# A fifth token tile's normalised rows turned by VectorE and DRAM scratch instead of TensorE, with the turned rows of both halves in blocks of 32 tokens

## The chip, the cores and the metric

The kernel runs on one core of a Trainium2 chip (trn2). The time is device microseconds of one execution of the whole program; the time before is the median of three runs. A profiled execution, taken separately, gives the trace from which all rows below come.

## What is computed

One decoder layer on 1024 tokens (plus 16 meta tokens in front) of width 1024, float32. Cut to what matters here:

```
u = rmsnorm(h, g_pre_mix);  q, k, v, xr, yr = split(u @ w_in)
attn = sliding_window_attention(q, k, v);  rec = gelu(yr) * rg_lru(conv(xr))
h = h + rmsnorm(concat(attn, rec) @ w_out, g_post_mix)       # "output projection"
u = rmsnorm(h, g_pre_ffn)                                    # "second norm"
f = square(relu(u @ w_ff1)) @ w_ff2                          # d_ff = 4096
return h + rmsnorm(f, g_post_ffn)
```

The change concerns the second norm's result `u`, on its way from rows (a token per partition) to columns (a feature per partition), as the product with `w_ff1` needs it.

## The kernel before

**Products.** Each float32 product is made of three TensorE products of rounded parts (`mm3`, lines 123-133): high by high (line 125), high by low (line 130), low by high (line 131). The high part is a ScalarE cast and the low part a VectorE subtraction (`split`, lines 94-101: casts at line 96, subtractions at line 99). Both feed-forward products are done with a seven-product scheme on 2x2 blocks, so sums and differences of blocks of `u` and of the weights have to be formed first (`combine`, line 1029).

**The output projection and the second norm, lines 1136-1188.** The tokens go in eight tiles of 128 rows, t = 0 to 7. For each t, `out_mm` makes two TensorE banks; `out_norm` squares them on ScalarE (line 972), takes a root on GpSimd (`rstd_of`, lines 167-179), scales them on VectorE (line 978), adds x (line 981), writes h to the output (line 982, SyncE's DMA queue), and gets the second norm's factor (lines 984-985). `out_scale` then follows one or two tiles later (`scale_at`, line 1142).

- For t = 0 to 3, `u2_store` scales by the norm's factor and by `g_pre_ffn` in one VectorE instruction that also deals the columns out (line 930), turns the 32x32 blocks by a VectorE transpose (line 937), and stores 512 KB to a DRAM scratch `u2_dram` (line 938, SyncE's queue). `u2_read` (lines 940-945), one step of the loop later, reads it back in four loads of 128 KB into the four tiles `u2f[0]`, of shape [128, 16, 2, 32]: 16 blocks of 32 tokens, each with 2 feature chunks.
- For t = 4 to 7, `out_scale` scales the rows alone (line 991), and `u2_tiles` (lines 994-1017) turns them by eight TensorE transposes against an identity (line 1003). They go from PSUM to the four tiles `u2f[1]`, of shape [128, 2, 512], by four ScalarE instructions (line 1014) and two VectorE instructions (line 1008), which multiply by `g_pre_ffn`; for t = 6 ScalarE does all eight.

**After the turn.** `b11` and `b21` are the split parts of `u2f[0]` (lines 1183, 1186). `t_sums` (lines 1156-1161) forms `t3 = u2f[1][2+i] - u2f[1][i]` and `t2 = t3 + u2f[0][i]` and splits `t2` into `ot2`. It is called for tiles 4 and 5 (line 1178), 6 (line 1195) and 7 (line 1198). The function `rows` (lines 1031-1034) views a plain [128, 2, 512] tile by blocks of 32 tokens where the other operand is in blocks.

**The first feed-forward product.** `p1` and `p2` (lines 1146-1154) do the products that need only `u2f[0]`, for four blocks of weights. Then a loop over 16 blocks p of `w_ff1` begins (line 1224): `prep_a` (lines 1060-1083) loads two tiles of 512 KB by SyncE's queue (lines 1062 and 1064; `raw` and `a` or `d` tiles), forms sums (line 1029), and splits a part into `ws` and a part into `e` tiles; `product(ya[p], wa[p][1], ot2, ...)` (line 1229) uses `ot2`, and a store to DRAM scratch leaves by GpSimd's queue (line 1082).

**The order of the work.** A scheduler puts the instructions of each engine, and the DMA issues of SyncE, into one fixed order when the kernel is built; every engine then runs its own list in that order, waiting on semaphores. `behind` adds order constraints by hand. A wait therefore holds up all that stands behind it on that engine or queue. One tile pool has two `e` buffers (one holds `gmix_b` through this stage) and two `raw` buffers.

Of the kernel before, what the change touches and what calls it, by code (L numbers as in the profile page):

```python
# [9 lines left out]
F32 = mybir.dt.float32  # L10
F32R = mybir.dt.float32r
AF = mybir.ActivationFunctionType
ALU = mybir.AluOpType
# [3 lines left out]
P = 128  # L17
# [20 lines left out]
def hybrid_layer(  # L38
# [14 lines left out]
    dpool = ctx.enter_context(tc.tile_pool(name="dpool", bufs=1, space=DRAM))  # L53
# [4 lines left out]
    def slot(tag, shape, dt=F32):  # L58
        uid[0] += 1
        return slab.tile(shape, dt, tag=tag, name=f"{tag}{uid[0]}", bufs=bufs[tag])  # L60

    def pair(tag, shape):
        return slot(tag, shape, F32R), slot(tag, shape, F32R)

    def bank(tag, shape=(P, 512)):
        uid[0] += 1
        return ps.tile(list(shape), F32, tag=tag, name=f"ps_{tag}{uid[0]}")

    def f32(ap):
        return ap.bitcast(F32)  # L70
# [23 lines left out]
    def split(hi, lo, src, eng=None):  # L94
        if eng is None:
            nc.scalar.copy(hi, src)  # L96
        else:
            eng.tensor_copy(hi, src)
        low = nc.vector.tensor_tensor(lo, src, f32(hi), op=ALU.subtract).ins  # L99
        mark[0] = low.name  # L100
        return low


    mark = [None]

    def behind(name, *inss):
        for ins in inss:
            tc.add_manual_dep(
                ins, name,
                mybir.DependencyInfo(  # L110
                    mybir.DependencyClass.NoSync, mybir.DependencyReason.DATA
                ),
                reason="order",
            )
# [47 lines left out]
    g_mix_col, g_ffn_col = gcol[:, 0:8], gcol[:, 8:16]  # L162
# [368 lines left out]
    for h in range(2):  # L531
        r, o, m = HALF[h], HALF[1 - h], slice(P - NMETA, 2 * P)
# [62 lines left out]
    for b in range(2):  # L595
        pv = bank("pt", (P, 4, P))
        for i in range(4):
            o = NMETA + (4 * b + i) * P
# [319 lines left out]
    nc.scalar.dma_start(gmix_b, g_post_mix[0].partition_broadcast(P))  # L918
    t4_dram = dpool.tile([P, 2, 4, 512], F32, name="t4_dram")

    u2f = [[slot("c", [P, 16, 2, 32]) for _ in range(4)], [None] * 4]
    u2_dram = dpool.tile([4, 4, P, 2 * P], F32, name="u2_dram")
    gpre_b = slot("ws", [P, D])
    nc.scalar.dma_start(gpre_b, g_pre_ffn[0].partition_broadcast(P))

# [3 lines left out]
    def u2_store(t, h, rs, tmp):  # L929
        ins = nc.vector.scalar_tensor_tensor(  # L930
            tmp.rearrange("p (b k d) -> p k d b", b=4, k=KC), dealt(h), rs,
            dealt(gpre_b), op0=ALU.mult, op1=ALU.mult,
        ).ins
        if t < 3:
            behind(summed[t + 1], ins)
        y = slot("e", [P, D])
        nc.vector.transpose(y, tmp)
        nc.sync.dma_start(u2_dram[t].rearrange("a (d b) r -> (a d) (b r)", b=4), y)

    def u2_read(t):  # L940
        for q in range(4):
            nc.sync.dma_start(
                u2f[0][q][:, 4 * t : 4 * t + 4].rearrange("p a k t -> p a (k t)"),
                u2_dram[t, :, :, 64 * q : 64 * q + 64].rearrange("a p r -> p a r"),
            )

    def out_mm(t, po, kcs):
        half, o = t // 4, (t % 4) * P
        s = slice(o, o + P)
        for n in range(2):  # L950
            c = slice(512 * n, 512 * n + 512)
            for kc in kcs:
                ah, al = at[half][kc // 2]
                mm3(
                    po[n], (ah[:, kc % 2, s], al[:, kc % 2, s]),
                    (wo[kc][0][:, c], wo[kc][1][:, c]), kc == 0, kc == KC - 1,
                )

    def out_banks(t):
        tag = ("pt", "o", "acc", "s", "pt", "acc", "s", "pt")[t]  # L960
        return [bank(tag), bank(tag)]
# [23 lines left out]
        return h, xr, rstd_of([ssq2])  # L985

    def out_scale(t, h, xr, rs2):
        if t < 4:
            u2_store(t, h, rs2, xr)
            return None  # L990
        nc.vector.tensor_scalar(xr, h, rs2, None, op0=ALU.mult)
        return xr

    def u2_tiles(t, xn):
        half = t // 4
        if u2f[half][0] is None:
            u2f[half] = [slot("c", [P, 2, 512]) for _ in range(4)]
        o = (t % 4) * P
        for k4 in range(0, KC, 4):
            pt = bank("o", (P, 4, P))  # L1000
            for i in range(4):
                kc = k4 + i
                nc.tensor.transpose(pt[:, i, :], xn[:, kc * P : (kc + 1) * P], ident)
            for i in range(0, 4, 2):
                kc = k4 + i
                dst = u2f[half][kc // 2]
                if k4 and t != 6:
                    nc.vector.tensor_tensor(
                        dst[:, :, o : o + P], pt[:, i : i + 2, :],
                        g_ffn_col[:, kc : kc + 2].to_broadcast([P, 2, P]), op=ALU.mult,  # L1010
                    )
                    continue
                for n in range(2):
                    nc.scalar.activation(
                        dst[:, n, o : o + P], pt[:, i + n, :], AF.Copy,
                        scale=g_ffn_col[:, kc + n : kc + n + 1],
                    )

    w1v = w_ff1.rearrange("(b k p) c -> b p k c", b=2, p=P)

# [4 lines left out]
    def combine(dst, x0, x1, op):  # L1028
        return nc.vector.tensor_tensor(dst, x0, x1, op=op).ins  # L1029

    def rows(t_, c=slice(0, 512)):
        if len(t_.shape) == 4:
            return t_[:, c.start // 32 : c.stop // 32]
        return t_[:, :, c].rearrange("p k (g t) -> p g k t", t=32)

    def operand(tiles):
        pairs = []
        for t_ in tiles:
            hi, lo = pair("b", [P, 2, 512])
            if len(t_.shape) == 4:  # L1040
                split(rows(hi), rows(lo), t_)
            else:
                split(hi, lo, t_)
            pairs.append((hi, lo))
        return pairs

# [39 lines left out]
    def early(b, p0, hl, tag="raw"):  # L1086
        raw = slot(tag, [P, 2, 4, P])
        for k in range(2):
            w1_load(raw[:, k], b, p0 + k, 0, 1)
        split(*hl, raw)  # L1090
        return {p0 + k: (hl[0][:, k], hl[1][:, k]) for k in range(2)}
# [63 lines left out]

    def t_sums(c):
        for i in range(2):
            combine(t3[i][:, :, c], u2f[1][2 + i][:, :, c], u2f[1][i][:, :, c], ALU.subtract)
            combine(rows(t2[i], c), rows(t3[i], c), rows(u2f[0][i], c), ALU.add)
            hi, lo = ot2[i]  # L1160
            split(hi[:, :, c], lo[:, :, c], t2[i][:, :, c])

    for t in range(8):
        po = pos[t] if t < 4 else out_banks(t)
        out_mm(t, po, range(6 if t < 4 else 0, KC))
        if t > 5:
            u2_tiles(t - 2, xns[t - 2])
        if t == 7:
            t3 = [slot("a", [P, 2, 512]) for _ in range(2)]
            t2 = [slot("a", [P, 2, 512]) for _ in range(2)]  # L1170
            ot2 = [pair("b", [P, 2, 512]) for _ in range(2)]
        halfway[t] = out_norm(t, po)
        for k in scale_at[t]:
            xns[k] = out_scale(k, *halfway.pop(k))
        if 1 <= t <= 4:
            u2_read(t - 1)
        if t == 7:
            t_sums(slice(0, 2 * P))
            u2_tiles(6, xns[6])
        if t == 4:  # L1180
            a11_early.update(early(0, 0, pair("a", ESH)))
        if t == 5:
            b11 = operand(u2f[0][0:2])
            a12_early.update(early(1, 0, pair("ws", ESH)))
        if t == 6:
            b21 = operand(u2f[0][2:4])
            hl = slot("b", ESH, F32R), slot("e", ESH, F32R)
            a11_early.update(early(0, 2, hl))
# [3 lines left out]
        p1(p, a11_early[p])  # L1192
    for p in range(2):
        p2(p, a12_early[p])
    t_sums(slice(2 * P, 3 * P))
    wa[0] = prep_a(0)
    u2_tiles(7, xns[7])
    t_sums(slice(3 * P, 4 * P))
    urgent = mark[0]
    for p in range(2, 4):  # L1200
        p1(p, a11_early[p])
    p2(2, a12_early[2])
    ot3 = [pair("b", [P, 2, 512]) for _ in range(2)]
    for i in range(2):
        behind(urgent, split(*ot3[i], t3[i]))
    token_low = mark[0]
    wa[1] = prep_a(1, urgent)

# [1 line left out]
    def t_rest(k):  # L1210
        i = k % 2
        if k < 2:
            behind(mark[0], combine(rows(u2f[1][i]), rows(u2f[1][i]), u2f[0][i], ALU.subtract))
        elif k < 4:
            behind(mark[0], combine(rows(t2[i]), u2f[0][2 + i], rows(t2[i]), ALU.subtract))
        else:
            hl = pair("a", [P, 2, 512])
            late = mark[0]
            behind(late, split(*hl, t2[i]))
            for n in range(2):  # L1220
                nc.gpsimd.dma_start(t4_dram[:, n, 2 * i : 2 * i + 2, :], f32(hl[n]))

# [277 lines left out]
    for n, (i, q) in enumerate(steps):  # L1500
# [3 lines left out]
        if n + 1 < len(steps):  # L1504
            late = w_low[0]
# [55 lines left out]
```

## Time and profile before

| | us |
|---|---|
| median of 3 runs (949.52 to 950.42) | 950.23 |
| the profiled execution's own time | 949.03 |
| its span, first to last instruction | 947.3 |
| granted TensorE clock, share of full | 0.998 |

The page of the profile gives busy time by engine, the chain of work that ended last, and the costliest groups. The timeline gives instructions in order of time: start, duration, engine, line, operation, what is written and read (buffer numbers left out), and in square brackets how long the engine sat idle before and what released it. PE is TensorE, DVE VectorE, ACT ScalarE, POOL GpSimd, SPq SyncE's queue of DMA issues. A matmul's duration includes its pipeline: the distance from one start to the next is what it costs. Line numbers are those of the kernel before.

### The profile page before, as it was taken

The numbers are of one execution on the slowest core, as the hardware profiler recorded it, in microseconds if no ns is written. First come the engines' busy times: TensorE is split into PE (matmuls) and PEld (weight loads), VectorE is DVE, ScalarE is ACT, GpSimd is POOL, SyncE is SP. The second block draws the span as 40 slices with busy tenths as digits, with TensorE's granted clock in tenths as the row PEclk, the third lists the DMA queues.
The fourth block names the chain that finished last, engine by engine and source line by source line (L and its number), as shares of the span: only waits on it lengthen the run. The fifth ranks groups of instructions, "written<-read, shape, count | busy, mean of one in ns | idle before, by whom it ended". The sixth has DMA issues, their size and how long they took to land.

```text
span 947.3 us, 12174 instructions
## 1 busy us (share of the span) xinstructions
PE 937.9 (99%) x4584; PEld 784.8 (83%) x4584; DVE 664.4 (70%) x849; ACT 505.0 (53%) x844; POOL 135.9 (14%) x205
## 2 busy tenths in 40 slices
PE   9999999999999999999999999999999999999996
PEld 8999999878888878888888888888888888888885
DVE  6667788779977987665544465476667676779783
ACT  8546765569634664443655575654533443445441
POOL 4104437431021100010000000001111000001201
PEclk9999999999999999999999999999999999999999
DMA  8220011104259658574422363334777655537934
GB/s 273 57 68 23 24 45 45 45 23 141 82 194 273 200 180 283 188 258 134 156 89 89 111 215 120 109 111 114 198 170 178 206 179 192 194 126 209 238 64 89
DMA packets 97366, 134.91 MB, mean 142 GB/s; under 512 B 22230, under 2 KB 61158, under 8 KB 97308
## 3 DMA queue, kind: packets, MB, share of 16 engines
q1 hardware_dynamic: 87996, 108.64, 35.3%
q0 software_dynamic: 8880, 24.19, 11.9%
q10 hardware_dynamic: 432, 1.31, 0.4%
q8 instruction: 36, 0.59, 0.3%
q14 instruction: 22, 0.18, 0.1%
HBM read 112.55 MB, written 20.97 MB: 141 GB/s over the span
## 4 chain that ended last, share of the span: by engine, by line
PE 97%; DVE 1%; DMA 0%; ACT 0%; issue 0%; SPq 0%; DVEq 0%
PE ps_acc L125 12%; PE ps_acc L131 12%; PE ps_acc L130 12%; PE ps_pt L131 6%; PE ps_s L131 6%; PE ps_pt L125 6%; PE ps_pt L130 6%; PE ps_s L125 6%; PE ps_s L130 6%; PE ps_o L125 5%; PE ps_o L131 5%; PE ps_o L130 5%; PE ps_o L697 2%; PE ps_acc L282 1%; PE ps_s L629 1%; PE ps_s L633 1%
## 5 line engine op out<-in xcount | busy, mean ns | idle before, releaser
L99 DVE TENSOR_TENSOR ws<-raw,ws 128x1024 fp32r<-128x1024 f32 (+1 forms) x69 | 82.3, 1193 | 72.4 <-PE ps_o L130 23.1
L96 ACT CAST ws<-raw 128x1024 fp32r<-128x1024 f32 (+1 forms) x68 | 69.8, 1027 | 82.0 <-PE ps_o L130 33.6
L96 ACT CAST ws<-e 128x1024 fp32r<-128x1024 f32 x41 | 43.0, 1050 | 85.8 <-PE ps_o L130 38.2
L130 PE MATMUL ps_acc<-a,ws 128*128 128x512 f32 (+3 forms) x240 | 82.9, 346 | 0.0
L125 PE MATMUL ps_acc<-a,ws 128*128 128x512 f32 (+3 forms) x240 | 82.8, 346 | 0.0
L131 PE MATMUL ps_acc<-a,ws 128*128 128x512 f32 (+3 forms) x240 | 82.2, 343 | 0.0
L99 DVE TENSOR_TENSOR b<-b,b 128x1024 fp32r<-128x1024 f32 (+2 forms) x50 | 59.0, 1179 | 27.9 <-PE ps_o L130 22.6
L99 DVE TENSOR_TENSOR ws<-e,ws 128x1024 fp32r<-128x1024 f32 x41 | 50.2, 1223 | 31.7 <-ACT ws L96 18.4
L96 ACT CAST b<-b 128x1024 fp32r<-128x1024 f32 (+2 forms) x49 | 50.0, 1020 | 41.8 <-DVE b L1029 35.5
L684 POOL TENSOR_SCALAR_AFFINE_SELECT c<-c 128x512 fp32r<-128x512 f32 x64 | 55.0, 873 | 73.7 <-ACT c L96 64.2
L125 PEld LDWEIGHTS ps_acc<-a,ws 128*128 128x128 f32 x240 | 45.2, 189 | 4.3 <-issue 0.7
L131 PEld LDWEIGHTS ps_acc<-a,ws 128*128 128x128 f32 x240 | 45.2, 188 | 3.7 <-issue 0.2
L130 PEld LDWEIGHTS ps_acc<-a,ws 128*128 128x128 f32 x240 | 45.2, 188 | 3.6 <-issue 0.4
L131 PE MATMUL ps_acc<-ws,b 128*128 128x512 f32 (+1 forms) x120 | 46.3, 386 | 0.0
L130 PE MATMUL ps_acc<-ws,b 128*128 128x512 f32 (+1 forms) x120 | 46.2, 385 | 0.0
L125 PE MATMUL ps_acc<-ws,b 128*128 128x512 f32 (+1 forms) x120 | 46.0, 385 | 0.0
L125 PE MATMUL ps_pt<-ws,b 128*128 128x512 f32 x112 | 44.3, 395 | 0.0
L131 PE MATMUL ps_pt<-ws,b 128*128 128x512 f32 x112 | 44.2, 395 | 0.0
L130 PE MATMUL ps_pt<-ws,b 128*128 128x512 f32 x112 | 44.1, 394 | 0.0
L131 PE MATMUL ps_s<-ws,b 128*128 128x512 f32 x110 | 43.4, 394 | 0.0
L130 PE MATMUL ps_s<-ws,b 128*128 128x512 f32 x110 | 43.4, 394 | 0.0
L125 PE MATMUL ps_s<-ws,b 128*128 128x512 f32 x110 | 43.3, 394 | 0.0
(417 smaller groups left out, 2660.0 us busy)
## 6 DMA issues: line engine op xcount, KB each, us to landing
raw<-in_w_ff_dram SPq DMA_DIRECT2D x59, 512.0 KB, 3.9
e<-in_w_ff_dram SPq DMA_DIRECT2D x43, 512.0 KB, 3.5
a<-in_w_ff_dram SPq DMA_DIRECT2D x12, 512.0 KB, 6.0
s_dram<-a POOLq DMA_DIRECT2D x12, 512.0 KB, 4.1
raw<-in_w_in_dram SPq DMA_DIRECT2D x9, 512.0 KB, 3.6
c<-in_x_dram SPq DMA_DIRECT2D x8, 512.0 KB, 4.5
d<-in_x_dram SPq DMA_DIRECT2D x8, 512.0 KB, 3.4
out_dram<-raw SPq DMA_DIRECT2D x8, 512.0 KB
```

The source lines that it names most:

```text
L96: nc.scalar.copy(hi, src)
L99: low = nc.vector.tensor_tensor(lo, src, f32(hi), op=ALU.subtract).ins
L125: ins = nc.tensor.matmul(dst, lh, rh, start=start, stop=False, skip_group_check=True).ins
L130: nc.tensor.matmul(dst, lh, rl, start=False, stop=False, skip_group_check=True)
L131: last_mm[0] = nc.tensor.matmul(dst, ll, rh, start=False, stop=stop, skip_group_check=True).ins.name
L282: last_mm[0] = nc.tensor.matmul(acc[:, :n], w[k // 2][:, kc, :], u[kc][k % 2][:, t0 : t0 + n], start=k == 0 and kc == 0, stop=k == last an ...
L629: nc.tensor.matmul(dst, q[h][:, c], hi, start=True, stop=False, skip_group_check=True,)
L633: nc.tensor.matmul(dst, q[h][:, c], lo, start=False, stop=True, skip_group_check=True,)
L684: nc.gpsimd.affine_select(out=p_[:, :, s], in_=f32(p_[:, :, 0]), pattern=[[0, 4], [g, P]], compare_op=op, fill=0.0, base=0, channel_multip ...
L697: nc.tensor.matmul(two[:, :, oc : oc + w], v, p_.rearrange("p (j i) s c -> p j (i s c)", j=2)[:, :, pc : pc + w], start=n == 0 and k == 0, ...
```

## The change

Tile t = 4 goes the way of tiles 0 to 3: `out_scale` calls `u2_store` for t < 5, the scratch has five parts, and `u2_read(4)` is called in the loop's step 5. `u2_tiles` is called for tiles 5, 6 and 7 only. All four tiles `u2f[1]` are now allocated together with `u2f[0]`, with the same shape [128, 16, 2, 32] in blocks of 32 tokens; `t2` and `t3` have that shape too. So the sums (line 1029) run over plain, equal layouts, and the split into `ot2`, `ot3` and the later operands goes through the view `rows`. `u2_tiles` writes its results into blocks of 32 tokens.

```
+    MOVED = 5
+    u2f = [[slot("c", [P, 16, 2, 32]) for _ in range(4)] for _ in range(2)]
+    u2_dram = dpool.tile([MOVED, 4, P, 2 * P], F32, name="u2_dram")
...
     def u2_read(t):
...
-                u2f[0][q][:, 4 * t : 4 * t + 4].rearrange("p a k t -> p a (k t)"),
+                u2f[t // 4][q][:, 4 * (t % 4) : 4 * (t % 4) + 4].rearrange(
+                    "p a k t -> p a (k t)"
+                ),
...
     def out_scale(t, h, xr, rs2):
-        if t < 4:
+        if t < MOVED:
             u2_store(t, h, rs2, xr)
...
     def u2_tiles(t, xn):
+            pt = pt.rearrange("p k (a t) -> p k a t", t=32)
...
-                dst = u2f[half][kc // 2]
+                dst = by_k(u2f[1][kc // 2][:, o : o + 4])
...
     def operand(tiles):
-            if len(t_.shape) == 4:
-                split(rows(hi), rows(lo), t_)
-            else:
-                split(hi, lo, t_)
+            split(rows(hi), rows(lo), t_)
...
     def t_sums(c):
         for i in range(2):
-            combine(t3[i][:, :, c], u2f[1][2 + i][:, :, c], u2f[1][i][:, :, c], ALU.subtract)
-            combine(rows(t2[i], c), rows(t3[i], c), rows(u2f[0][i], c), ALU.add)
+            combine(t3[i][:, c], u2f[1][2 + i][:, c], u2f[1][i][:, c], ALU.subtract)
+            combine(t2[i][:, c], t3[i][:, c], u2f[0][i][:, c], ALU.add)
             hi, lo = ot2[i]
-            split(hi[:, :, c], lo[:, :, c], t2[i][:, :, c])
+            split(rows(hi, c), rows(lo, c), t2[i][:, c])
...
-        if t > 5:
+        if t > MOVED + 1:
             u2_tiles(t - 2, xns[t - 2])
...
-            t3 = [slot("a", [P, 2, 512]) for _ in range(2)]
-            t2 = [slot("a", [P, 2, 512]) for _ in range(2)]
+            t3 = [slot("a", [P, 16, 2, 32]) for _ in range(2)]
+            t2 = [slot("a", [P, 16, 2, 32]) for _ in range(2)]
...
-        if 1 <= t <= 4:
+        if 1 <= t <= MOVED:
             u2_read(t - 1)
...
-        behind(urgent, split(*ot3[i], t3[i]))
+        behind(urgent, split(*map(rows, ot3[i]), t3[i]))
```

The scheduler's fixed orders of the two builds, compared instruction by instruction:

- TensorE: the eight transposes of tile 4 are gone. Those of tile 6 stand 2 products earlier, those of tile 7 stand 10 products later than before: between them and the first product with `ot2` there were 15 products, now there are 5. A few of `p1`'s products for p = 2 and 3 are exchanged with one another and with `p2`'s, and some 160 products further on one pair stands 12 earlier.
- VectorE: in tile 4's place, lines 930 and 937 for lines 991 and 1008. In `t_sums` for tiles 4 and 5, one scaling (line 991, tile 6) stands ahead of two sums instead of behind them. In `t_sums` for tile 7, one addition of `p2` (line 1154) stands between the two pairs of sums instead of behind the first low part.
- ScalarE: four instructions of line 1014 are gone.
- SyncE's queue: the store of tile 4 stands behind the output of tile 5; its four reads stand behind the next weight load. Of the two tiles that `prep_a(3)` loads, the `raw` tile stands ahead of the `a` tile instead of behind it, and the `a` tile for p = 4 behind both.
- GpSimd: the same list.

More of the change, by code (lines that the diff above doesn't have):

```diff
@@ L919, in hybrid_layer @@
     t4_dram = dpool.tile([P, 2, 4, 512], F32, name="t4_dram")
-    u2f = [[slot("c", [P, 16, 2, 32]) for _ in range(4)], [None] * 4]
-    u2_dram = dpool.tile([4, 4, P, 2 * P], F32, name="u2_dram")
+    MOVED = 5
+    u2f = [[slot("c", [P, 16, 2, 32]) for _ in range(4)] for _ in range(2)]
+    u2_dram = dpool.tile([MOVED, 4, P, 2 * P], F32, name="u2_dram")
     gpre_b = slot("ws", [P, D])
@@ L992, in out_scale, with by_k @@
         return xr
+    def by_k(t_):
+        return t_.rearrange("p a k t -> p k a t")
     def u2_tiles(t, xn):
[L995 to L998, printed above, removed]
+        o = 4 * (t % 4)
         for k4 in range(0, KC, 4):
@@ L1003, in u2_tiles @@
                 nc.tensor.transpose(pt[:, i, :], xn[:, kc * P : (kc + 1) * P], ident)
+            pt = pt.rearrange("p k (a t) -> p k a t", t=32)
             for i in range(0, 4, 2):
                 kc = k4 + i
-                dst = u2f[half][kc // 2]
+                dst = by_k(u2f[1][kc // 2][:, o : o + 4])
                 if k4 and t != 6:
                     nc.vector.tensor_tensor(
-                        dst[:, :, o : o + P], pt[:, i : i + 2, :],
-                        g_ffn_col[:, kc : kc + 2].to_broadcast([P, 2, P]), op=ALU.mult,
+                        dst, pt[:, i : i + 2],
+                        g_ffn_col[:, kc : kc + 2].rearrange(
+                            "p (k a t) -> p k a t", a=1, t=1
+                        ).to_broadcast([P, 2, 4, 32]),
+                        op=ALU.mult,
                     )
@@ L1014, in u2_tiles @@
                     nc.scalar.activation(
-                        dst[:, n, o : o + P], pt[:, i + n, :], AF.Copy,
+                        dst[:, n], pt[:, i + n], AF.Copy,
                         scale=g_ffn_col[:, kc + n : kc + n + 1],
@@ L1029, in combine, with rows @@
         return nc.vector.tensor_tensor(dst, x0, x1, op=op).ins
-    def rows(t_, c=slice(0, 512)):
-        if len(t_.shape) == 4:
-            return t_[:, c.start // 32 : c.stop // 32]
-        return t_[:, :, c].rearrange("p k (g t) -> p g k t", t=32)
+    def rows(t_, c=slice(0, 16)):
+        return t_[:, :, 32 * c.start : 32 * c.stop].rearrange("p k (a t) -> p a k t", t=32)
     def operand(tiles):
@@ L1039, in operand @@
             hi, lo = pair("b", [P, 2, 512])
-            if len(t_.shape) == 4:
-                split(rows(hi), rows(lo), t_)
-            else:
-                split(hi, lo, t_)
+            split(rows(hi), rows(lo), t_)
             pairs.append((hi, lo))
@@ L1174, in hybrid_layer @@
             xns[k] = out_scale(k, *halfway.pop(k))
-        if 1 <= t <= 4:
+        if 1 <= t <= MOVED:
             u2_read(t - 1)
         if t == 7:
-            t_sums(slice(0, 2 * P))
+            t_sums(slice(0, 8))
             u2_tiles(6, xns[6])
@@ L1194, in hybrid_layer @@
         p2(p, a12_early[p])
-    t_sums(slice(2 * P, 3 * P))
+    t_sums(slice(8, 12))
     wa[0] = prep_a(0)
     u2_tiles(7, xns[7])
-    t_sums(slice(3 * P, 4 * P))
+    t_sums(slice(12, 16))
     urgent = mark[0]
@@ L1212, in t_rest @@
         if k < 2:
-            behind(mark[0], combine(rows(u2f[1][i]), rows(u2f[1][i]), u2f[0][i], ALU.subtract))
+            behind(mark[0], combine(u2f[1][i], u2f[1][i], u2f[0][i], ALU.subtract))
         elif k < 4:
-            behind(mark[0], combine(rows(t2[i]), u2f[0][2 + i], rows(t2[i]), ALU.subtract))
+            behind(mark[0], combine(t2[i], u2f[0][2 + i], t2[i], ALU.subtract))
         else:
@@ L1218, in t_rest @@
             late = mark[0]
-            behind(late, split(*hl, t2[i]))
+            behind(late, split(*map(rows, hl), t2[i]))
             for n in range(2):
```

## The prediction

> **What bounds the kernel now.** I read the page's chain first, then the timeline of TensorE through the stage that changes, looking for starts further apart than the rest, then the busy times of that stage.
>
> ```profile
> PE 97%; DVE 1%; DMA 0%; ACT 0%; issue 0%; SPq 0%; DVEq 0%
> ```
>
> The chain that ended last is 97% TensorE: products back to back. So a TensorE instruction that goes is worth its spacing, and everything else counts only if it makes TensorE wait. In the changed stage TensorE waits in one place, seen where two starts stand 0.47 and 0.34 apart:
>
> ```profile
> 345.45 0.40 PE L130 MATMUL ps_s<-b,e 128*128 128x512 f32 x1
> 345.92 0.51 PE L131 MATMUL ps_acc<-b,e 128*128 128x512 f32 x1
> 346.26 0.40 PE L125 MATMUL ps_acc<-b,e 128*128 128x512 f32 x1
> ```
>
> Behind it I found no two starts over 0.31 us apart to the end. VectorE, which feeds TensorE here, has little room between tile 5's turn and this place:
>
> ```profile
> 314.00:346.00 32.00, 31.93 (x151) 25.79 (x149) 29.68 (x53) 23.21 (x49) 4.49 (x7) 1.00 0.63 198
> 346.00:366.00 20.00, 20.00 (x87) 16.22 (x88) 12.71 (x19) 8.45 (x13) 1.72 (x4) 1.00 0.89 289
> ```
>
> The columns after the length are busy us of PE, PEld, DVE, ACT and POOL, then the granted clock. VectorE is busy 29.68 of 32.00 us in the first stretch and 12.71 of 20.00 in the next. So TensorE is the bound, with VectorE close behind up to 346, and the question is whether the new order keeps VectorE in time.
>
> **Step 1, the transposes that go.** Tile 4's eight transposes:
>
> ```profile
> 302.27 1.04 PE L1003 MATMUL ps_o<-ident,d 128*128 128x128 f32 x8
> 303.06 0.48 PE L125 MATMUL ps_pt<-ws,b 128*128 128x512 f32 x1
> 303.38 0.40 PE L130 MATMUL ps_pt<-ws,b 128*128 128x512 f32 x1
> ```
>
> From 302.27 to 303.38 are 1.11 us for the transposes and one product; a product's spacing is 0.23 (worked out in step 4). That is **-0.88 us**, on the path.
>
> **Step 2, what VectorE does instead.** One row per operation (min/median/max ns):
>
> ```profile
> L930 DVE SCALAR_TENSOR_TENSOR d<-raw,rs,ws x4: 2036/2103/2118, 270.5 to 287.7; 128x1024 f32<-128x1024 f32 x4
> L937 DVE STREAM_TRANSPOSE e<-d x4: 1236/1245/1247, 272.7 to 293.1; 128x1024 f32<-128x1024 f32 x4
> L991 DVE TENSOR_SCALAR d<-raw,rs x4: 753/754/755, 295.4 to 326.8; 128x1024 f32<-128x1024 f32 x4
> L1008 DVE TENSOR_TENSOR c<-ps_o,gcol x6: 414/419/425, 303.3 to 333.4; 128x256 f32<-128x256 f32 x6
> ```
>
> VectorE gains 2.10 + 1.25 and loses 0.75 + 2 x 0.42: +1.76 us. The cover is its idle time at that place:
>
> ```profile
> 303.34 0.76 DVE L1008 TENSOR_TENSOR c<-ps_o,gcol 128x256 f32<-128x256 f32 x2 [1.50 <-PE ps_o L1003]
> 304.07 0.75 DVE L991 TENSOR_SCALAR d<-raw,rs 128x1024 f32<-128x1024 f32 x1
> 305.32 1.23 DVE L99 TENSOR_TENSOR ws<-raw,ws 128x1024 fp32r<-128x1024 f32 x1 [0.50 <-ACT ws L96]
> ```
>
> The 1.50 waited for transposes that are gone, the 0.50 for a cast that stood behind the four ScalarE instructions that are gone. 2.00 of idle time against 1.76: I cost it at nothing; without that cover VectorE would be 1.76 late for tile 5.
>
> **Step 3, the scratch.** SyncE's queue around it, the landing of such reads, and the first sum of `t_sums`:
>
> ```profile
> 299.69 3.77 SPq L942 DMA_DIRECT2D c<-u_dram  x4
> 303.56 0.55 SPq L982 DMA_DIRECT2D out_dram<-raw  x1
> 307.32 0.92 SPq L1026 DMA_DIRECT2D raw<-in_w_ff_dram  x2
> c<-u_dram SPq DMA_DIRECT2D x16, 128.0 KB, 3.7
> 315.98 0.68 DVE L1029 TENSOR_TENSOR a<-c,c 128x512 f32<-128x512 f32 x1
> ```
>
> The turn takes line 1008's place on VectorE and ends near 303.3, so the store goes behind the output, at about 304.1. The weight load behind went at 307.32, and I leave it there. The four reads follow from 308.24, one each 0.94 at the slowest spacing shown (3.77 / 4). The first sum needs the first and the third: the third goes at 310.1 and lands 3.7 later, 313.8. The sum cannot start before 315.98 - 0.88 = 315.1. In time by 1.3 us, so I cost it at nothing; a read must take over 5 us to make VectorE wait. The Trainium skill (VectorE: DVE Perf Modes, The three transpose paths) warns that a plain DMA copy which turns by strides is 19 times slower than the crossbar's transpose. By it 512 KB would take some 25 us (an estimate from its 19, at 90% of the 435 GB/s fabric ceiling in DMA: Bandwidth & Descriptors, Specifications). The 3.7 us row, with the same blocks, says that this doesn't hold: the 32x32 turn is VectorE's, and the copy moves runs.
>
> **Step 4, tile 7 and the first product with `ot2`.** This decides the forecast.
>
> ```profile
> 331.99 1.03 PE L1003 MATMUL ps_o<-ident,d 128*128 128x128 f32 x8
> ...
> 336.58 0.39 PE L130 MATMUL ps_acc<-b,e 128*128 128x512 f32 x1
> ```
>
> ```profile
> 333.07 0.76 DVE L1008 TENSOR_TENSOR c<-ps_o,gcol 128x256 f32<-128x256 f32 x2
> 333.74 0.75 DVE L1029 TENSOR_TENSOR a<-c,c 128x256 f32<-128x256 f32 x2
> 334.40 0.76 DVE L1029 TENSOR_TENSOR a<-a,c 128x256 f32<-128x256 f32 x2
> 335.63 0.42 DVE L99 TENSOR_TENSOR b<-a,b 128x256 fp32r<-128x256 f32 x1 [0.47 <-ACT b L96]
> 336.55 0.69 DVE L1154 TENSOR_TENSOR b<-ps_pt,b 128x512 f32<-128x512 f32 x1 [0.50 <-PE ps_pt L131]
> ```
>
> Call the start of tile 7's transposes X. Before, X = 331.99 and the high-by-low product, the first that needs the low part of `ot2`, starts at X + 4.59: the transposes' 0.88 and 16 products, so (4.59 - 0.88) / 16 = 0.23 each. The low part is ready at 336.05 = X + 4.06: in time by half a microsecond. In the new order the transposes stand 10 products later, X = 331.99 - 0.88 + 2.32 = 333.43, and only 6 products lie between: TensorE would be there at X + 0.88 + 1.39 = X + 2.27. VectorE's chain is not shorter: line 1008 at X + 1.08, the first sums at X + 1.75, then line 1154, which now stands between (0.69 by its row, some 0.6 to the next start, as the pairs of 0.75 take 0.66 to the next), the second sums at X + 3.0, their first half written 0.42 later, a cast, for which I take 0.42 too, and the low part of 0.42: X + 4.35 with the hand-overs. TensorE waits 4.35 - 2.27 = **+2.08 us**. Both ends: without line 1154's 0.60 and no worse cast, X + 4.06 less 2.27, 1.8; if VectorE itself comes late to tile 7, more by as much, though X stands 1.44 later than before and VectorE, there without idle time at 333.07, has that much more room. I put the upper end at 3.3. The layouts themselves cost nothing: the pair of sums at 333.74 runs over plain operands and the one at 334.40 over one in blocks, 0.75 and 0.76.
>
> TensorE is then at 331.99's old schedule by -0.88 + 2.08 = +1.20.
>
> **Step 5, the old wait at 345.45 goes.** Two products took 0.81 there instead of 0.46. Between tile 7 and that place VectorE has the same list but for exchanges: it comes later by tile 7's 1.44, less the 0.47 and 0.50 that it waited in the rows above, +0.47. TensorE comes 1.20 later, so it no longer waits: **-0.35 us**. If VectorE came 1.20 late too, the wait would stay.
>
> **Step 6, the loads of `prep_a(3)`.**
>
> ```profile
> 332.31 1.75 SPq L1026 DMA_DIRECT2D a<-in_w_ff_dram  x2
> 345.89 9.45 SPq L1026 DMA_DIRECT2D raw<-in_w_ff_dram  x3
> ```
>
> ```profile
> 345.18 0.69 DVE L99 TENSOR_TENSOR e<-raw,e 128x512 fp32r<-128x512 f32 x1
> ...
> 350.87 0.69 DVE L1029 TENSOR_TENSOR a<-raw,a 128x512 f32<-128x512 f32 x1 [3.20 <-DMA raw<-in_w_ff_dram]
> ...
> 357.99 1.23 DVE L99 TENSOR_TENSOR ws<-raw,ws 128x1024 fp32r<-128x1024 f32 x1 [1.72 <-ACT ws L96]
> ```
>
> ```profile
> 359.48 0.39 PE L131 MATMUL ps_acc<-b,ws 128*128 128x512 f32 x1
> a<-in_w_ff_dram SPq DMA_DIRECT2D x12, 512.0 KB, 6.0
> d<-in_w_ff_dram SPq DMA_DIRECT2D x8, 512.0 KB, 8.1
> L96 ACT CAST ws<-raw 128x1024 fp32r<-128x1024 f32 (+1 forms) x68 | 69.8, 1027 | 82.0 <-PE ps_o L130 33.6
> ```
>
> The two `a` tiles were issued at 332.31 and long there; the `raw` tile, whose buffer the low part at 345.18 frees, at 345.89. Now the `a` tiles queue behind that `raw` issue: it waits until 345.89 + 0.47, about 346.4, the first `a` tile goes half a microsecond behind (0.92 for two issues at 307.32) and lands 6.0 later, 352.9. VectorE starts on p = 3 then instead of at 350.87. From that start to the low part for `p1` of p = 4 it has the same eight instructions: 357.99 - 350.87 - 1.72 = 5.40, then a cast (1.03) and the low part (1.23), 7.8 with hand-overs: 360.7. TensorE wants it at 359.48 + 1.20 - 0.35 = 360.33. **+0.35 us**. Bounds: 0 if the tile lands within 5.6; if it takes 8.1, the median of the `d` tiles, 2.4. The Trainium skill (DMA: Bandwidth & Descriptors, Queues, rings and completion order) says that descriptors of one queue are consumed in ring order and that engines take turns between queues; by that the loads queued behind do not slow this one, and it speaks for the low end.
>
> **Sum.** -0.88 + 2.08 - 0.35 + 0.35 = +1.20 against the profiled execution's 949.03: 950.23; against the median of the runs, which lies 1.20 above that execution, 950.23 + 1.20 = **951.4 us**. That is 0.13%, and about 0.2% (1.9 us) is what a measurement of this kernel can tell from no change.
>
> **The rivals.**
>
> *Only the transposes count.* If VectorE's chain for tile 7 keeps up, -0.88 - 0.35 = -1.2: 949.0. For it: TensorE's 97%. Against it: the chain took 4.06 us before and has 2.27. Chance 0.12.
>
> *SyncE's queue decides (slower).* The `a` tile behind the waiting `raw` issue lands late, among six transfers of 512 KB where there were four. It costs one for one from a landing at 352.5 on, and turns the change into a measurable loss from 353.6; at 8.1 us after issue the sum is 1.20 + 2.05: 953.5. For it: the 8.1 of the `d` tiles. Against it: the median 6.0. Chance 0.22.
>
> *The reads of tile 4 come late.* Then VectorE stands in front of `t_sums`, with the scaling of tile 6 and all sums behind it; over 2.7 us of lateness (1.3 of margin, 1.4 of room at tile 7) TensorE waits one for one. At 5 us beyond the 3.7: 951.4 + 2.3 = 953.7. Against it: the 3.7 of 16 such reads. Chance 0.06. The rule of step 3 on strided copies would be the extreme of this case; it has no chance of its own.
>
> That the transposes stay is excluded by the lists of instructions.
>
> **How the numbers follow.** Forecast as summed, 950.4 to 952.1: 0.58. With the first rival (within 0.2% too) 0.70 for the same; slower by over 0.2% 0.28 (second and third rival); faster 0.02, since no more than 1.23 us can be gained on TensorE here. The range runs from the first rival to the second, 949.0 to 953.6.
>
> **What would show it.** Right: eight transposes fewer; a gap of about 2 us on TensorE between tile 7's last `p2` product and the second product with `ot2`, ended by VectorE's line 99; no gap near 346; SyncE issuing both `a` tiles near 347 and VectorE idle until about 353. Wrong: no gap at `ot2`, or VectorE idle ahead of `t_sums` for a read, or tile 7's transposes themselves late.

## The result, and the profile after

| | median, us | runs | against before |
|---|---|---|---|
| before | 949.68 (949.43 to 950.42) | 6 | |
| changed | 952.54 (952.01 to 954.14) | 6 | ratio 1.0032, 95% interval 1.0021 to 1.0044 |
| changed, a second time | 952.70 (952.04 to 953.15) | 9 | 1.0029, 1.0019 to 1.0039 (before beside it: 949.76) |

The changed kernel is slower by 2.86 us, 0.3%, and the interval lies wholly above 0.2%. That is inside the stated range, but it is not the forecast case (+1.20): it is nearer to the second rival (1.20 + 2.05 = +3.25). The kernel before came out at 949.68, 0.55 below the median that the forecast stood on, so 952.54 looks nearer to the forecast 951.4 than the change itself is to +1.20.

Two profiled executions differ in more than the change. To compare stages I take the distance between two TensorE instructions that stand outside the changed part, one of the mixing layers and one in the long rows of products behind. Before:

```profile
259.02 0.50 PE L131 MATMUL ps_pt<-a,b 128*128 128x512 f32 x1
...
554.38 1.99 PE L1280 MATMUL ps_pt<-b,ws 128*128 128x512 f32 x8
```

After (line 1279 is before's 1280):

```profile
259.75 0.50 PE L131 MATMUL ps_pt<-a,b 128*128 128x512 f32 x1
...
557.87 1.99 PE L1279 MATMUL ps_pt<-b,ws 128*128 128x512 f32 x8
```

295.36 us before, 298.12 after: **+2.76 us in this stretch**, which is the difference of the medians to 0.1 us. The trace after is 0.73 us later already at the first row, so 0.73 goes off when a row after is set beside one of before.

The page's chain after:

```profile
PE 93%; DMA 2%; DVE 2%; ACT 1%; issue 0%; POOL 0%; SPq 0%; DVEq 0%; ACTq 0%; POOLq 0%
```

TensorE's share falls from 97% to 93%: DMA, VectorE and ScalarE have come into the chain, so TensorE now waits for them. The timeline of TensorE after shows where, first at tile 7:

```profile
334.19 1.04 PE L1006 MATMUL ps_o<-ident,d 128*128 128x128 f32 x8
...
335.99 0.40 PE L131 MATMUL ps_pt<-b,a 128*128 128x512 f32 x1
338.21 0.50 PE L125 MATMUL ps_acc<-b,e 128*128 128x512 f32 x1 [1.82 <-ACT b L96]
338.67 0.50 PE L130 MATMUL ps_acc<-b,e 128*128 128x512 f32 x1
```

Between 335.99 and 338.21 TensorE stands idle for 1.82 us, for the high part of `ot2`; the next product, which needs the low part, starts at 338.67. Before it started at 336.58, so TensorE is 338.67 - 336.58 - 0.73 = 1.36 us late here. The second place:

```profile
358.24 0.40 PE L130 MATMUL ps_s<-b,e 128*128 128x512 f32 x1
359.91 0.50 PE L131 MATMUL ps_s<-b,e 128*128 128x512 f32 x1 [1.28 <-DVE e L99]
```

Here it waits 1.28 us for the low part of p = 3's `e` tile, which the product with `ot2` needs. SyncE's queue and VectorE around p = 3 show why:

```profile
331.21 16.44 SPq L1030 DMA_DIRECT2D raw<-in_w_ff_dram  x3
347.69 1.35 SPq L1030 DMA_DIRECT2D a<-in_w_ff_dram  x2
349.16 11.09 SPq L1030 DMA_DIRECT2D raw<-in_w_ff_dram  x2
```

```profile
354.56 0.69 DVE L1033 TENSOR_TENSOR a<-raw,a 128x512 f32<-128x512 f32 x1 [5.51 <-DMA a<-in_w_ff_dram]
...
358.56 0.69 DVE L1033 TENSOR_TENSOR a<-raw,a 128x512 f32<-128x512 f32 x1 [0.59 <-DMA raw<-in_w_ff_dram]
359.17 0.69 DVE L99 TENSOR_TENSOR e<-raw,e 128x512 fp32r<-128x512 f32 x1
```

The first row of SyncE's queue is a group of three issues of `raw` that ends at 347.65, since the third waits for its buffer; only then go the two `a` tiles, which before went at 332.31. VectorE stands 5.51 us for the first of them. The load behind them, at 349.16, is `raw` for p = 4, and VectorE stands another 0.59 us for it at 358.56, the first sum of p = 4. The low part that TensorE waits for comes only behind that sum, at 359.17. In the kernel before it stands ahead of it:

```profile
354.26 0.68 DVE L99 TENSOR_TENSOR e<-raw,e 128x512 fp32r<-128x512 f32 x1
354.86 0.69 DVE L1029 TENSOR_TENSOR a<-raw,a 128x512 f32<-128x512 f32 x1
```

So VectorE's order has changed here too, which the comparison of the two builds ahead of the prediction does not have.

One more thing stands earlier on VectorE:

```profile
326.90 1.23 DVE L99 TENSOR_TENSOR a<-a,a 128x1024 fp32r<-128x1024 f32 x1 [1.40 <-ACT a L96]
...
335.37 0.75 DVE L1012 TENSOR_TENSOR c<-ps_o,gcol 128x256 f32<-128x256 f32 x2
```

The first row waits for ScalarE's cast of the `a` tile of the weights' early load, whose issue had slipped behind a `raw` issue too (319.47; before 315.73). The second is tile 7's eviction, with no wait ahead of it: the transposes were ready 1.08 us behind their start by the prediction's measure, at 335.27, and VectorE came at 335.37. So at `ot2` two things are late together, the transposes and VectorE itself.

### The profile page after: what moved, and what is told of

Same layout as the page of the kernel before. It is cut to its first block, busy times and chain, and to the rows that moved or that the text cites. A ratio compares the mean times of both kernels' runs of the same rounds, so it can differ in the third digit from the quotient of the medians.

```text
span 952.0 us, 12166 instructions
## 1 busy us (share of the span) xinstructions
PE 938.4 (99%) x4576; PEld 783.8 (82%) x4576; DVE 666.3 (70%) x848; ACT 504.3 (53%) x840; POOL 136.0 (14%) x205
## 4 chain that ended last, share of the span: by engine, by line
PE 93%; DMA 2%; DVE 2%; ACT 1%; issue 0%; POOL 0%; SPq 0%; DVEq 0%; ACTq 0%; POOLq 0%
PE ps_acc L125 11%; PE ps_acc L131 11%; PE ps_acc L130 11%; PE ps_pt L131 6%; PE ps_pt L125 6%; PE ps_pt L130 6%; PE ps_s L131 6%; PE ps_s L125 6%; PE ps_s L130 6%; PE ps_o L130 5%; PE ps_o L131 5%; PE ps_o L125 5%; PE ps_o L697 2%; PE ps_acc L282 1%; DMA raw<-in_w_ff_dram 1%; PE ps_s L629 1%
```

## The experiments

The theory from these rows: the layout and VectorE's added work cost nothing, and the loss is made of orders that the scheduler changed by the way: tile 7's transposes (step 4), SyncE's queue around p = 3 (step 6), and the early `a` load. The rival: the layout or the added work. All runs, with the medians' difference against the kernel before on the same chip and the stretch of the trace as above:

| run | median, us | against before, us | ratio, 95% interval | stretch, against 295.36 |
|---|---|---|---|---|
| e1_blocks_only | 949.99 | +0.12 | 0.9991 to 1.0009 | -0.01 |
| e2_a_first | 951.56 | +1.69 | 1.0007 to 1.0024 | +1.36 |
| e3_tile7_first | 950.22 | +0.35 | 0.9996 to 1.0014 | +0.45 |
| e5_before_raw_first | 952.19 | +2.32 | 1.0014 to 1.0033 | +2.32 |
| after_again | 952.70 | +2.94 | 1.0019 to 1.0039 | +2.96 |
| e10_tile7_queue_kept | 952.87 | +3.11 | 1.0019 to 1.0041 | +3.17 |
| e11_early_queue_kept | 952.38 | +2.62 | 1.0019 to 1.0039 | +2.60 |
| e9_early_tile7 | 949.78 | +0.02 | 0.9990 to 1.0008 | +0.31 |
| e12_low_first | 948.85 | -0.94 | 0.9979 to 0.9997 | -0.87 |

The kernel before was 949.87 beside the first four, 949.76 beside the next four and 949.79 beside the last. Medians and stretches agree within 0.35 us throughout.

### The layout alone

```
-    MOVED = 5
+    MOVED = 4
...
-        if t > MOVED + 1:
+        if t > 5:
```

> The changed kernel with four tiles moved instead of five: tile 4's rows are turned by TensorE again, and only the layout in blocks of 32 tokens is left of the change. TensorE's and SyncE's orders are those of the kernel before. Theory (two queues' orders make the loss): the layout costs nothing, 949.7 us, within 0.5 of the kernel before, and no wait of TensorE above 1 us at the first high-by-low product with the tiles ot2. Rival (the layout costs: the sums in t_sums, their splits and the evictions read and write rows of 32 elements instead of 128 and delay tile 7's part): 0.5 to 1.5 us above the kernel before, and the sums and splits of 1,024 to 4,096 elements longer than their 0.69 and 0.70 us of before.

Measured: 949.99, and the stretch is that of before to 0.01 us. The sums of `t_sums` took 417 to 420 ns in the median (before 421 to 424). The layout costs nothing, and that half of the rival falls. The added work stays in all other runs made from the changed kernel, and the last of them shows what it costs.

### The `a` tile of p = 3 ahead of `raw`

```
-        w1_load(r0, 0, p, 0, 2)
+        low_half = w1_load(r0, 0, p, 0, 2)
...
-        w1_load(r1, 1, p, 0, 2)
+        high_half = w1_load(r1, 1, p, 0, 2)
+        if p == 3:
+            behind(high_half.name, low_half)
```

> The changed kernel with one edge more in the order: the load of raw for p = 3 stands behind the load of a for p = 3 on SyncE's queue. The orders of the four computing engines are those of the changed kernel. The changed kernel waited 5.51 us on VectorE for that a tile, which went at 347.69 behind raw at 347.27, and TensorE then 1.28 us for the low part, with 0.3 more behind. Theory (the place in the queue makes this wait): a goes near 334, VectorE starts p = 3 when raw lands, about 352.5, TensorE's wait at ps_s<-b,e goes, about 1.6 us less than the changed kernel: 1.2 us above the kernel before, 950.9. Rival (it is the traffic at 347 to 356, not the place): raw itself lands at 354 or later, the wait only changes its name, and the time stays 2.9 above the kernel before, 952.5.

Measured: 951.56, 1.2 us less than the changed kernel by the medians (2.86 - 1.69), 1.4 by the stretch. SyncE's queue and VectorE in this run:

```profile
333.32 0.56 SPq L1030 DMA_DIRECT2D a<-in_w_ff_dram  x1
346.77 2.22 SPq L1030 DMA_DIRECT2D raw<-in_w_ff_dram  x2
```

```profile
352.50 0.69 DVE L1033 TENSOR_TENSOR a<-raw,a 128x512 f32<-128x512 f32 x1 [3.96 <-DMA raw<-in_w_ff_dram]
```

The `a` tile goes at 333.32, VectorE now waits for `raw` and starts p = 3 at 352.50 instead of 354.56 (0.40 of it is the trace's: its first row of the stretch stands at 259.35). TensorE's wait of 1.28 us at `ps_s<-b,e` is gone but for two starts 0.41 apart. The place in the queue made the second wait; the traffic rival, which had `raw` landing at 354 or later, falls.

### The queue alone, put into the kernel before

```
+        low_half = w1_load(r0, 0, p, 0, 2)
+        high_half = w1_load(r1, 1, p, 0, 2)
+        if p == 3:
+            behind(low_half.name, high_half)
```

> The kernel before with the loads of a for p = 3 and 4 behind the load of raw for p = 3 on SyncE's queue, as the changed kernel has them; twelve-product groups of p = 3 on TensorE change places, none is added. Theory (the queue alone makes a loss): the a tile goes near 346.4 instead of 332.31 and lands 6.0 to 6.8 later, 352.4 to 353.2, VectorE starts p = 3 1.5 to 2.3 later than at 350.87, and TensorE, which is not late here by anything else, waits for it: 1.0 to 2.0 us above the kernel before, 950.7 to 951.7. Rival (the step is hidden, VectorE has slack there): within 0.5 of the kernel before, 949.7.

Measured: 952.19, +2.32, more than expected. VectorE, SyncE's queue and TensorE there:

```profile
353.36 0.69 DVE L1029 TENSOR_TENSOR a<-raw,a 128x512 f32<-128x512 f32 x1 [5.20 <-DMA a<-in_w_ff_dram]
358.63 0.69 DVE L1029 TENSOR_TENSOR a<-raw,a 128x512 f32<-128x512 f32 x1 [1.26 <-DMA raw<-in_w_ff_dram]
```

```profile
346.80 1.42 SPq L1026 DMA_DIRECT2D a<-in_w_ff_dram  x2
348.33 9.43 SPq L1026 DMA_DIRECT2D raw<-in_w_ff_dram  x2
```

```profile
361.18 0.50 PE L125 MATMUL ps_acc<-b,ws 128*128 128x512 f32 x1 [1.14 <-ACT ws L96]
```

With all eight transposes of tile 4, tile 7's in their old place, and no work added, this one exchange in SyncE's queue, with groups of products of p = 3 exchanged on TensorE, makes most of the loss of the change. The wait of 1.14 falls on `ps_acc<-b,ws`, the first part for p = 4, where the prediction had put it. VectorE waits twice, 5.20 us for `a` of p = 3 and 1.26 us for `raw` of p = 4, which went at 348.33 behind both `a` tiles. The expectation had only the first of these waits.

### Tile 7's transposes earlier

```
-                nc.tensor.transpose(pt[:, i, :], xn[:, kc * P : (kc + 1) * P], ident)
+                last_tr[0] = nc.tensor.transpose(
+                    pt[:, i, :], xn[:, kc * P : (kc + 1) * P], ident
+                ).ins.name
...
-    p2(2, a12_early[2])
+    p2(2, a12_early[2], last_tr[0])
```

> The changed kernel with tile 7's eight transposes tied ahead of the twelve products of p2 for p = 2, seven products (2.4 us) earlier than the changed kernel has them. Rival one, the prediction's step 4 as it stands (the transposes' place alone makes the gap of about 2.3 us at ot2): the gap goes, and with it 2 us, 950.4 if the wait for p = 3's low part does not grow. Theory (VectorE was late as well: it came to tile 7's eviction at 335.37 without a wait, because the a tile of the second half's early load was 1.40 us late for it): the gap shrinks by less than 0.5, and what it shrinks is waited again at ps_s<-b,e, whose time comes from SyncE's queue: 2.4 to 2.9 above the kernel before, 952.1 to 952.6.

Measured: 950.22, near the first rival's 950.4. But this run did two things. With the transposes in another place the scheduler also put both `a` loads of p = 3 and 4 at 333.84, ahead of `raw` at 347.19, as in the kernel before. My theory had taken SyncE's queue for fixed. So the same edit was made again with the queue held:

```
+        if 3 <= p <= 4:
+            behind(low_half[3].name, high_half)
```

> The changed kernel with tile 7's transposes seven products earlier, as in the run that gained 2.3 us by it, but now with SyncE's queue held to the changed kernel's order around p = 3 (the loads of a for p = 3 and 4 behind that of raw for p = 3; in the other run the planner had put them in front by itself). Theory (the two waits stand one behind the other, and the later one sets the time): the gap at ot2 shrinks from 2.35 to about 1.2 us, but the low part of p = 3 comes at the same time as before, since its a tile goes behind raw at about 347.2, so TensorE waits about 2.8 us there instead of 1.6: 2.4 to 2.9 above the kernel before, 952.5. Rival (the waits add up): the 1.2 us at ot2 are gained, 1.5 above the kernel before, 951.4.

Measured: 952.87, no gain at all. TensorE's two waits in this run:

```profile
337.30 0.50 PE L125 MATMUL ps_acc<-b,e 128*128 128x512 f32 x1 [1.34 <-ACT b L96]
338.14 0.50 PE L130 MATMUL ps_acc<-b,e 128*128 128x512 f32 x1 [0.34 <-DVE b L99]
359.90 0.50 PE L131 MATMUL ps_s<-b,e 128*128 128x512 f32 x1 [1.64 <-DVE e L99]
```

The wait at `ot2` becomes 1.34 and 0.34 instead of 1.82, and the one at `ps_s<-b,e` grows from 1.28 to 1.64. Counted from the first row of the stretch, the third row comes 100.57 us later (359.90 - 259.33), in the changed kernel 100.16 (359.91 - 259.75): not earlier. The low part comes when the loads of SyncE's queue let it come, and whatever TensorE gains ahead of it, it waits for there. The waits do not add up.

### The early load earlier, the queue around p = 3 kept

```
+            early_load[0] = w1_load(raw[:, k], b, p0 + k, 0, 1).name
...
+        if 3 <= p <= 4:
+            behind(low_half[3].name, high_half)
+        if p == 0:
+            behind(early_load[0], low_half[0])
```

(The function meant is `early`, lines 1086 to 1091 of the kernel before, in its last call.)

> The changed kernel with the load of the second half's early a tile (lines 1066 and 1084 of the kernel before: early, called for p = 2 and 3) ahead of p = 0's raw on SyncE's queue, as the kernel before has it, and with the queue around p = 3 as the changed kernel has it; the planner then puts tile 7's transposes two products earlier. Theory (of the 2.35 us at ot2 about half is VectorE's own lateness, which comes from this load's place): VectorE's wait of 1.40 us at line 99 (a<-a,a) goes, the gap at ot2 shrinks to 1.2 to 1.7, since the transposes still stand 5 products too late, and p = 3's raw is issued up to 1 us earlier, so that the later wait shrinks as well: 1.2 to 2.0 above the kernel before, 951.0 to 951.9. Rival (VectorE's lateness does not matter): within 0.4 of the changed kernel, 952.6.

Measured: 952.38, within 0.4 of the changed kernel, as the rival had it. The early load did what it should: VectorE's 1.40 went and the wait at `ot2` fell to 0.93. The wait at `ps_s<-b,e` grew to 1.75. p = 3's `raw` went at 347.20 instead of 347.27, not 1 us earlier: VectorE had lost its lead again in front of tile 7's transposes, for which it now waited 1.35 us. VectorE's lateness was real and cost nothing of its own.

### The changed kernel again

> The changed kernel itself once more, beside the three experiments, as their yardstick: 2.5 to 3.1 us above the kernel before, as measured first (2.86), and in the trace 2.5 to 2.9 us more than before between the last product ps_pt<-a,b of the mixing layers and the long row of products of line 1279.

Measured: 952.70, +2.94, stretch +2.96. One thing is not as in the first trace: there is no wait at `ps_s<-b,e`. In its place the clock fell, behind the wait at `ot2`:

```profile
338.49 0.50 PE L125 MATMUL ps_acc<-b,e 128*128 128x512 f32 x1 [2.02 <-ACT b L96]
```

```profile
339.00:341.00 2.00, 2.00 (x7) 0.70 0.00 1
341.00:342.00 1.00, 1.00 (x4) 0.50 0.00 0
342.00:343.00 1.00, 1.00 (x4) 0.50 0.00 0
343.00:344.00 1.00, 1.00 (x5) 0.89 0.00 0
```

The columns of the second view, after the length, are TensorE's busy us and instructions, then the granted clock. At half clock TensorE lost about 1.6 us (21 instructions from 340 to 346, in the first trace 28; 7 x 0.23), and came to `ps_s<-b,e` when the low part was there. The total is the same within 0.2: again the later event sets the time.

### All orders put back

The two edits for the early load and for tile 7's transposes together; the scheduler then puts the `a` loads of p = 3 and 4 in front by itself.

> The changed kernel with all that it moved by the way put back: the early a tile ahead of p = 0's raw, tile 7's transposes seven products earlier, and (the planner does it by itself then) the loads of a for p = 3 and 4 ahead of raw for p = 3. TensorE keeps the eight transposes fewer. Theory (transposes -0.88, everything else a matter of order): the gap at ot2 goes, no wait at ps_s<-b,e, 0.6 to 1.0 us below the kernel before, 949.0. Rival (VectorE's added work of tile 4, 4.1 us ahead of tile 7's rows, keeps it late): a gap of 0.5 to 1.2 us at ot2 stays, 949.7 to 950.2, no gain over the kernel before.

Measured: 949.78, no gain over the kernel before; the rival's range. TensorE and VectorE in this run:

```profile
336.52 0.44 PE L125 MATMUL ps_acc<-b,e 128*128 128x512 f32 x1
337.80 0.50 PE L130 MATMUL ps_acc<-b,e 128*128 128x512 f32 x1 [0.84 <-DVE b L99]
```

```profile
335.27 0.76 DVE L1037 TENSOR_TENSOR a<-a,c 128x256 f32<-128x256 f32 x2
336.72 0.69 DVE L1161 TENSOR_TENSOR b<-ps_pt,b 128x512 f32<-128x512 f32 x1 [0.69 <-PE ps_pt L131]
337.33 1.89 DVE L99 TENSOR_TENSOR b<-a,b 128x256 fp32r<-128x256 f32 x3
```

The high part is in time now. The low part is not: the sums end at 336.03, but the addition of `p2`'s product stands ahead of the low part on VectorE and waits 0.69 us for TensorE. That is an order again, not a lack of speed, so one more edge. A second one holds the `a` tile of p = 3 ahead of its `raw`, where it already stood in this run:

```
+        if p == 3:
+            behind(high_half.name, low_half)
...
+        total = nc.vector.tensor_tensor(block("11", p), y2, block("11", p), op=ALU.add).ins
+        if p == 2:
+            behind(urgent, total)
```

> The version with all three orders put back (949.78, no gain over the kernel before) and one thing more: on VectorE the addition of p2's product for p = 2 (b<-ps_pt,b, which waited 0.69 us for TensorE at 336.72 ahead of tile 7's low parts) stands behind those low parts, as it stands behind the first of them in the kernel before. Theory (the 0.84 us at ot2 that were left come from this place in VectorE's order): the gap shrinks to 0.3 or less and the time to that of the eight transposes fewer, 0.6 to 0.9 us below the kernel before, 949.0, which lies inside what a measurement can tell. Rival (VectorE's chain behind tile 7's transposes is late in any order): the gap stays at 0.6 us or more, 949.6 to 949.9.

Measured: 948.85, ratio 0.9988 (0.9979 to 0.9997), faster than both kernels. That is less than the 0.2% that the prediction took for the limit of a measurement, but the interval lies below 1, and the stretch says the same:

```profile
259.80 0.50 PE L131 MATMUL ps_pt<-a,b 128*128 128x512 f32 x1
...
554.29 1.99 PE L1293 MATMUL ps_pt<-b,ws 128*128 128x512 f32 x8
```

294.49 us: 0.87 less than before, the size of the eight transposes (0.88). Two small terms nearly cancel: the starts at `ot2` still stand 0.40 and 0.34 apart, and the old pair near 346 now stands 0.33 and 0.33 apart instead of 0.47 and 0.34.

```profile
336.25 0.44 PE L125 MATMUL ps_acc<-b,e 128*128 128x512 f32 x1
336.65 0.50 PE L130 MATMUL ps_acc<-b,e 128*128 128x512 f32 x1
336.99 0.39 PE L131 MATMUL ps_acc<-b,e 128*128 128x512 f32 x1
```

So VectorE's added work, the turn of tile 4, costs TensorE nothing that can be seen here. In this build the scheduler also put the low part of p = 3 ahead of p = 4's first sum again, as in the kernel before; in the run ahead of this one it stood behind that sum, and TensorE did not wait there either. VectorE at `ot2`:

```profile
336.17 0.76 DVE L99 TENSOR_TENSOR b<-a,b 128x256 fp32r<-128x256 f32 x2 [0.41 <-ACT b L96]
336.85 0.68 DVE L1163 TENSOR_TENSOR b<-ps_pt,b 128x512 f32<-128x512 f32 x1
```

## Why the prediction was right and wrong

**Step 1, right.** Tile 5's transposes start at 314.08 after (before 314.24): 314.08 - 0.73 - 314.24 = -0.89, against -0.88. In the last experiment the whole gain is of this size.

**Step 2, right.** The added work stands where the prediction put it, and the sums of `t_sums` begin without a wait, as a row of step 3 shows.

```profile
303.55 1.24 DVE L938 STREAM_TRANSPOSE e<-d 128x1024 f32<-128x1024 f32 x1
305.87 0.75 DVE L994 TENSOR_SCALAR d<-raw,rs 128x1024 f32<-128x1024 f32 x1 [1.08 <-POOL rs L176]
```

VectorE even stands 1.08 us idle behind the turn, for GpSimd's root. The first sum starts 316.82 - 0.73 - 315.98 = 0.11 us later than before: the added work is covered to 0.1 us.

**Step 3, right.** The store went at 305.21 (1.1 later than put, 0.73 of it the trace's), the four reads together from 309.57:

```profile
309.57 2.27 SPq L943 DMA_DIRECT2D c<-u_dram  x4
```

```profile
316.82 0.68 DVE L1033 TENSOR_TENSOR a<-c,c 128x512 f32<-128x512 f32 x1
```

The first sum, on VectorE at 316.82, waited for nothing. By the nineteenfold price of strided copies that step 3 weighed (the Trainium skill, VectorE: DVE Perf Modes, The three transpose paths), some 25 us by the estimate there, it would have waited.

**Step 4, right in place and nearly in size.** X was to be 333.43, with 0.73 that is 334.16; the row says 334.19. TensorE was 1.36 us late behind the high-by-low product, against +1.20 forecast, so the gap was 2.24 instead of 2.08. Most of it stands one product earlier than I had put it, ended by ScalarE's cast of the high part (line 96) and not by VectorE's line 99: with the sums late, both parts are. What the step had wrong is VectorE's room. It gave it 1.44 us more, but VectorE came 0.10 behind the transposes, since the early `a` load had slipped on SyncE's queue; the step had weighed VectorE's list from tile 7 on and not what feeds the list before. In the changed kernel this cost 0.1; with the transposes earlier and the queue kept it held the gap at 1.34 and 0.34.

**Step 5, right.** Near 346 no two starts of TensorE stand over 0.24 us apart.

**Step 6, right in mechanism, wrong in size; the term that failed.** Forecast +0.35, measured about 1.6: the stretch's 2.76 less the 1.36 at `ot2` and a further 0.11 at the next start there, plus step 5's 0.35. The `a` tile went at 347.69, which less 0.73 is within 0.1 us of the step's place, but VectorE could use it only 354.56 - 347.69 = 6.87 us later, where 6.0 had been taken from the median of all loads of that kind. That is 0.9 of the missing 1.3. The rest comes from a wait that the step did not have: it gave VectorE eight instructions in a row behind the first `a` tile, but the first sum of p = 4 stood 0.59 us for its `raw` tile, issued behind both `a` tiles. In the kernel before that sum waited for nothing (the row at 354.86). The wait fell on p = 3's own low part, earlier in TensorE's list than the part for p = 4 that the step had compared, because VectorE now takes that sum ahead of the low part. No run tried this exchange by itself. Where the low part stood ahead of the sum, in the run with the queue alone, TensorE waited at p = 4 instead and the loss was 2.32: the exchange says where TensorE waits, the loads how long. The bounds, 0 to 2.4, held the 1.6, but not for this reason: they were made for the landing of one tile. The rule that the step weighed (the Trainium skill, DMA: Bandwidth & Descriptors, Queues, rings and completion order) was read there as speaking for the low end, loads queued behind do not slow this one. The runs go against that reading: `raw` of p = 3 reached VectorE 350.87 - 345.89 = 4.98 us after its issue before, and 352.50 - 346.77 = 5.73 us in the run with `a` of p = 3 in front, where one more load of 512 KB was issued behind it on the same queue.

**The sum.** Adding the steps was wrong in kind. With the queue as the change left it, taking the wait at `ot2` down gained nothing (952.87), and the queue's wait alone made 2.32. What could be gained at the gap of step 4 lay in the shadow of step 6; only with the queue put right does it show, 1.4 to 1.7 us above the kernel before with the saving of step 1 already taken off.

**The rivals.** The second, SyncE's queue, is what happened, at the 0.22 given to it. Its point of decision was a landing at 353.6; VectorE started on the tile at 354.56 - 0.73 = 353.83. The first rival's 949.0 is reached with the orders put back. The third did not come: no read of tile 4 was late.

## What to carry to other kernels

When a scheduler writes the order, compare each queue's list after an edit, and for every load that moves behind another ask what that other waits for: two loads behind one that waited for its buffer cost 2.3 us here, and the edit saved 0.88. Waits in a row do not add up: find the last one first, since nothing gained ahead of it counts until it is gone. Take a load's time from loads issued in the same crowd, not from a median over the program.

## What the runs showed of the hardware

- TensorE's granted clock fell to 0.50 behind the wait at `ot2` in one of two traces of the same kernel (2.02 us idle there), and stayed at 1.00 in the other (1.82 us idle). By the shares 0.70, 0.50, 0.50 and 0.89 in the rows above, the slow spell lasted 1.2 + 1 + 1 + 0.2 = 3.4 us. The Trainium skill (TensorE: Matmul & The Clock Gate, Why this matters for your kernels) asks for no idle gap over about 3 us; in this trace the fall came behind a gap of 2.02 us. That the gap made the clock fall is likely from its place, and no run tested it.
- A load of 512 KB issued directly behind another, with more behind it, was of use to VectorE 6.6 to 6.9 us after its issue in three runs (346.80 to 353.36, 347.69 to 354.56, and 347.76 to 354.57 in the run with the queue kept), against a median of 5.7 from issue to landing for the `a` tiles on the changed kernel's page. The load of 512 KB behind these was of use only 9.4 us after its issue (349.16 to 358.56); it was the fourth on the queue within 2 us.
